# Latent-token MLPs by one level of Strassen's scheme, the context MLP apart

## The chip, the cores and the metric

The kernel runs on one core of a Trainium2 chip. TensorE (PE) multiplies matrices into PSUM; VectorE (DVE), ScalarE (ACT) and GpSimd (POOL) work on tiles of 128 partitions in SBUF and PSUM; SyncE (SP) issues the DMAs between DRAM and SBUF. The metric is the device time of one execution in microseconds, less being better.

## The reference

Two layers of attention and MLP over 1024 latent tokens and 256 context tokens, with a width of 1024 and a hidden width of 4096, all in fp32. What the change concerns is the MLP of each layer (layer 0 also updates the context, layer 1 does not):

```python
def _mlp(h, w1, w2):
    a = jax.nn.relu(h @ w1)
    return (a * a) @ w2

# in reference(), per layer i, after the attention part
hx = hx + gx1 * yx
hx = hx + gx2 * _mlp(_modulate(hx, norm2_g[i], sx2, cx2), mlp_w1[i], mlp_w2[i])
if with_ctx:                      # layer 0 only
    hc = hc + gc1 * yc
    hc = hc + gc2 * _mlp(_modulate(hc, norm2_g[i], sc2, cc2), mlp_w1[i], mlp_w2[i])
```

`_modulate` is an RMS norm with a scale and a shift per channel.

## The kernel before

Activations are kept transposed, channels on partitions. The tokens are three tiles: latents 0 to 511 (tile 0), latents 512 to 1023 (tile 1) and the context (tile 2, 256 columns). Every fp32 matrix product is made of three matmuls on fp32r parts: each operand x is split into xh (a cast) and xl = x − xh, and `mm3` (L223 to 226) adds wh·xh, wh·xl and wl·xh. `wload` (L210 to 221) loads 512 KB of weights (tile wst), casts them on ScalarE (L219, wh) and subtracts on VectorE (L220, wl).

The MLP (`mlp`) takes the 32 hidden blocks of 128 in groups of two. For each tile of tokens, the first matrix is 24 matmuls per hidden block into a PSUM bank (pj); ScalarE applies ReLU (L323), VectorE squares (L325), ScalarE casts (L328, ah), VectorE subtracts (L329, al). The second matrix is, for each of the 8 output blocks, 6 matmuls (2 hidden blocks × 3) into a bank m, which VectorE scales by the gate and adds into h, held in SBUF (L349). `mlp_phase` orders the groups: in layer 0 the first four groups run tiles 0 and 2 while tile 1 is normed, in layer 1 tile 0 alone; the context goes along with the latents in layer 0 and uses the same loaded weights. The last two groups finish tile 0 ahead of the rest, so that its next norm (layer 0, `after0`) or its output (layer 1, `final`) overlaps with the others; layer 1's last group is cut into two column halves.

Ahead of each MLP, the out-projection of tile 1 (`out_proj0`, `out_proj_blk`) takes each block of h from DRAM (hc), adds and writes it back (hD), and `load_h` loads h again, 2 MB per tile (L790). After layer 0's MLP come the value projections of layer 1 (`v_part`), interleaved with the norms of tiles 1 and 2. During layer 0's MLP eight pieces of the next layer's conditioning (`ada_piece`) are computed.

A scheduler fixes each engine's order of instructions when the program is built, from the order in the code, priorities and a simulated time; pools of tiles with a fixed number of buffers set how far an engine may run ahead. All loads and stores are issued from SP's one queue, in its order.

## Time and profile before

| | us |
|---|---|
| median of 3 runs | 3144.76 (3142.53 to 3146.78) |
| span of the profiled execution | 3138.9 |
| PE busy | 3059.8 (97%) |
| VectorE busy | 1888.8 (60%) |
| ScalarE busy | 1263.7 (40%) |
| GpSimd busy | 266.3 (8%) |

The span runs from the first to the last instruction of one profiled execution. A timed run is 5.9 us longer in the median, for what lies around the span. The mean rate of the transfers is 115 GB/s. A share of busy time is a mean over stages: the views used below are the windows (busy time of each engine in a stretch), the groups by line, the chain of waits followed back from the last instruction, the timeline, and the list of DMA issues.

### The profile page before, as it was taken

The numbers are of one execution on the slowest core, as the hardware profiler recorded it, in microseconds if no ns is written. First come the engines' busy times: TensorE is split into PE (matmuls) and PEld (weight loads), VectorE is DVE, ScalarE is ACT, GpSimd is POOL, SyncE is SP. The second block draws the span as 40 slices with busy tenths as digits, with TensorE's granted clock in tenths as the row PEclk, the third lists the DMA queues.
The fourth block names the chain that finished last, engine by engine and source line by source line (L and its number), as shares of the span: only waits on it lengthen the run. The fifth ranks groups of instructions, "written<-read, shape, count | busy, mean of one in ns | idle before, by whom it ended". The sixth has DMA issues, their size and how long they took to land.

```text
span 3138.9 us, 45259 instructions
## 1 busy us (share of the span) xinstructions
PE 3059.8 (97%) x17346; PEld 2540.1 (81%) x17346; DVE 1888.8 (60%) x4317; ACT 1263.7 (40%) x2430; POOL 266.3 (8%) x262
## 2 busy tenths in 40 slices
PE   8999999999999999999999999999999999999998
PEld 5876767668888888888899888888887788888887
DVE  4456775766754445445671568997785755455455
ACT  5345664643321121121352236897784322211122
POOL 0100120300000000000000222322120000000000
PEclk9999999999999999999999999999999999999999
DMA  8478674441221111210334357655534231111122
GB/s 309 146 225 247 188 202 141 146 166 56 77 85 54 55 54 54 67 54 27 108 124 130 130 164 213 145 127 136 154 86 155 89 98 49 47 48 50 45 69 86
DMA packets 139768, 361.57 MB, mean 115 GB/s; under 512 B 16288, under 2 KB 41504, under 8 KB 138400
## 3 DMA queue, kind: packets, MB, share of 16 engines
q1 hardware_dynamic: 139552, 358.69, 37.2%
q8 instruction: 136, 2.23, 0.3%
q14 instruction: 80, 0.66, 0.1%
HBM read 297.81 MB, written 58.20 MB: 113 GB/s over the span
## 4 chain that ended last, share of the span: by engine, by line
PE 88%; DMA 5%; DVE 4%; ACT 1%; issue 1%; SPq 0%; POOL 0%; DVEq 0%; POOLq 0%; ACTq 0%
PE pj L224 12%; PE pj L226 12%; PE pj L225 12%; PE m L225 8%; PE m L224 8%; PE m L226 8%; PE s L938 4%; PE pv L979 4%; PE pvp L613 2%; PE pt L609 2%; PE pt L974 2%; PE op L224 2%; PE op L225 2%; PE op L226 2%; PE pv L309 2%; PE pv L310 2%
## 5 line engine op out<-in xcount | busy, mean ns | idle before, releaser
L224 PE MATMUL pj<-yh,wh 128*128 128x512 f32 (+1 forms) x1840 | 684.8, 373 | 14.1 <-DVE hc L657 4.4
L226 PE MATMUL pj<-yh,wl 128*128 128x512 f32 (+1 forms) x1840 | 684.1, 372 | 0.7 <-DVE wl L220 0.7
L225 PE MATMUL pj<-yl,wh 128*128 128x512 f32 (+1 forms) x1840 | 681.8, 371 | 0.5 <-DVE yl L254 0.5
L219 ACT CAST wh<-wst 128x1024 fp32r<-128x1024 f32 x274 | 285.3, 1049 | 930.3 <-PE m L225 536.7
L220 DVE TENSOR_TENSOR wl<-wst,wh 128x1024 fp32r<-128x1024 f32 x274 | 334.8, 1229 | 422.8 <-ACT wh L219 421.5
L349 DVE SCALAR_TENSOR_TENSOR h<-m,ada,h 128x512 f32<-128x512 f32 (+1 forms) x648 | 432.9, 689 | 185.7 <-PE m L226 182.0
L225 PE MATMUL m<-al,wh 128*128 128x512 f32 (+1 forms) x1296 | 474.6, 367 | 0.2 <-DVE al L329 0.2
L226 PE MATMUL m<-ah,wl 128*128 128x512 f32 (+1 forms) x1296 | 473.8, 366 | 0.0
L224 PE MATMUL m<-ah,wh 128*128 128x512 f32 (+1 forms) x1296 | 437.0, 368 | 5.2 <-ACT ah L328 5.2
L224 PEld LDWEIGHTS pj<-yh,wh 128*128 128x128 f32 x1840 | 349.7, 190 | 81.3 <-issue 6.9
L226 PEld LDWEIGHTS pj<-yh,wl 128*128 128x128 f32 x1840 | 349.6, 190 | 63.7 <-DVE wl L220 1.5
L225 PEld LDWEIGHTS pj<-yl,wh 128*128 128x128 f32 x1840 | 349.5, 190 | 62.1 <-DVE yl L254 0.8
L224 PEld LDWEIGHTS m<-ah,wh 128*128 128x128 f32 x1296 | 243.3, 189 | 46.7 <-ACT ah L328 6.5
L225 PEld LDWEIGHTS m<-al,wh 128*128 128x128 f32 x1296 | 245.5, 189 | 40.5 <-DVE al L329 0.4
L226 PEld LDWEIGHTS m<-ah,wl 128*128 128x128 f32 x1296 | 245.3, 189 | 40.0
L945 DVE CUSTOM_DVE_ANT_0 p<-s,zero 128x512 f32<-128x512 f32 (+1 forms) x384 | 213.4, 596 | 34.1 <-POOL p L967 19.0
L938 PE MATMUL s<-kt,qt 128*128 128x512 f32 (+1 forms) x768 | 196.3, 376 | 6.1 <-DVE m L945 4.7
L325 DVE TENSOR_TENSOR s<-r 128x512 f32<-128x512 f32 (+1 forms) x160 | 101.3, 634 | 153.5 <-ACT r L323 153.4
L957 ACT ACTIVATE p<-p,nm 128x1280 f32<-128x1280 f32 x128 | 175.2, 1369 | 33.8 <-DVE nm L956 33.4
L979 PEld LDWEIGHTS pv<-v,pT 128*128 128x128 f32 x1280 | 161.5, 191 | 18.0 <-ACT pT L976 12.7
L979 PE MATMUL pv<-v,pT 128*128 128x128 f32 x1280 | 172.7, 275 | 2.4 <-ACT pT L976 2.4
L323 ACT ACTIVATE r<-pj 128x512 f32<-128x512 f32 (+1 forms) x160 | 88.1, 551 | 194.8 <-PE pj L226 193.1
(152 smaller groups left out, 4322.9 us busy)
## 6 DMA issues: line engine op xcount, KB each, us to landing
wst<-in_mlp_w_dram SPq DMA_DIRECT2D x176, 512.0 KB, 3.5
adaw<-in_ada_w_dram SPq DMA_DIRECT2D x96, 512.0 KB, 5.6
kt<-kD SPq DMA_DIRECT2D x32, 640.0 KB, 9.9
q<-qD SPq DMA_DIRECT2D x64, 256.0 KB, 6.2
qt<-rD SPq DMA_DIRECT2D x64, 256.0 KB, 7.2
wst<-in_even_w_out_dram SPq DMA_DIRECT2D x24, 512.0 KB, 4.6
wst<-in_odd_qk_dram SPq DMA_DIRECT2D x24, 512.0 KB, 4.4
v<-vD SPq DMA_DIRECT2D x16, 640.0 KB, 4.0
```

The lines of the kernel that those rows point to most:

```text
L219: act.copy(wh, st)
L220: dve.tensor_tensor(wl, st, f32(wh), op=OP.subtract)
L224: pe.matmul(out, lhsT=wh, rhs=xh, start=first, stop=False)
L225: pe.matmul(out, lhsT=wh, rhs=xl, start=False, stop=False)
L226: pe.matmul(out, lhsT=wl, rhs=xh, start=False, stop=last)
L323: act.activation(r[:, :w], ps[:, :w], AF.Relu)
L325: dve.tensor_tensor(s[:, :w], r[:, :w], r[:, :w], op=OP.mult)
L349: dve.scalar_tensor_tensor(h[t][:, blk, c0:c1], ps[:, : c1 - c0], ada[layer][:, 40 + blk, c : c + 1], h[t][:, blk, c0:c1], op0=OP.mult, op ...
L938: pe.matmul(S[:, :cw], lhsT=q[n][:, m, sl], rhs=kt[:, m, c0 : c0 + cw], start=(n == 0), stop=(n == 1),)
L945: dve.tensor_tensor_reduce(p[:, c0 : c0 + cw], S[:, :cw], zero.to_broadcast([P, cw]), 1.0, 3e38, OP.add, OP.min, accum_out=m3[:, ci : ci + 1],
L957: act.activation(p, p, AF.Exp, bias=nm, scale=-1.0, accum_out=s2[:, m : m + 1])
L979: pe.matmul(pv, lhsT=pT[:, j * P : j * P + P], rhs=v[:, c, :], start=(c == 0), stop=(c == 9))
```

## The change

The latents' MLPs are written as one level of the Strassen-Winograd scheme, over a 2 × 2 split: the tokens by tile (0, 1), the inner dimension in halves, the hidden blocks in pairs. Seven block products take the place of eight; their operands are sums and differences of blocks (S1 to S4 of activations, T1 to T4 of weights), and the results are put together from the products in X, Y, Z.

First matrix: for each pair of hidden blocks seven products of 12 matmuls. The combinations of activations are made once per layer (`comb_split`); those of the weights per pair on GpSimd (L448 to 451, L456), and each combination is split by ScalarE (L433) and VectorE (L434, tile wp). For the first 8 pairs of a layer two products that need tile 0 alone run early (`early1`), while tile 1 is normed, and their results go through DRAM. After ReLU and square, GpSimd makes S1 to S4 (L545 to 549) and all seven operands of the pair are stored to DRAM, 256 KB each (aD, L553).

Second matrix (`mlp2`): in groups of four pairs, seven operands per pair are loaded again (sa, L570) and split; each product is 4 blocks × 12 matmuls. VectorE (L590) and ScalarE (L594, L595) evict them, and GpSimd adds the shared parts into h (L596, L600, L603). h is loaded at the joint between the matrices (L708). The first group's weight sums run on VectorE. Layer 1's last pair stays a plain second matrix, cut as before.

The context's MLP in layer 0 runs after the latents', with its own loads of all weights; its 8 output blocks stay in four PSUM banks until the end. The norms of tiles 0 and 1 for layer 1 run beside it, and the value stage is reordered. The out-projection of tile 1 adds into tiles of SBUF that the norm then reads. A weight buffer more (st 4 for 3), and a scratch size for dynamic DMA of 2048.

The diff, cut to its core:

```diff
+EARLY = 8
+GROUPS = ((0, 1, 2, 3), (4, 5, 6, 7), (8, 9, 10, 11), (12, 13, 14, 15))
+GROUPS_LAST = ((0, 1, 2, 3), (4, 5, 6, 7), (8, 9, 10, 11), (12, 13, 14))
...
-    def mlp_phase(layer, xs, first, rest, h, y, after, cuts=None):
...
+    ORDER = (
+        ("A11", "B11", "X", True),
+        ("S2", "T2", "Y", True),
+        ("A12", "B21", "X", False),
+        ("S1", "T1", "Z", True),
+        ("S3", "T3", "Y", False),
+        ("S4", "B22", "Z", False),
+        ("A22", "T4", "Y", False),
+    )
+    wturn, turn2 = [0], [1]
...
+    def split_pair(src, tag):
+        w = M.tile([P, 2, 512], F32R, name="wp", tag=tag)
+        act.copy(w[:, 0, :], src)
+        dve.tensor_tensor(w[:, 1, :], src, f32(w[:, 0, :]), op=OP.subtract)
+        return w
...
+    def wsums(B11, B12, B21, B22, eng=pool):
+        T3 = M.tile([P, 512], F32, name="tw")
+        eng.tensor_tensor(T3, B22, B12, op=OP.subtract)
+        T2 = M.tile([P, 512], F32, name="tw")
+        eng.tensor_tensor(T2, T3, B11, op=OP.add)
+        eng.tensor_tensor(B12, B12, B11, op=OP.subtract)
+        return {"B11": B11, "B21": B21, "B22": B22, "T1": B12, "T2": T2, "T3": T3}
+
+    def woperand(W, n):
+        if n == "T4":
+            pool.tensor_tensor(W["T2"], W["B21"], W["T2"], op=OP.subtract)
+            return wsplit(W["T2"])
+        return wsplit(W[n])
...
+    def product1(ps, w, comb, first):
+        hi, lo = comb
+        for k in range(4):
+            sl = slice(k * P, k * P + P)
+            wh, wl = w[:, 0, sl], w[:, 1, sl]
+            acc = dict(skip_group_check=True)
+            pe.matmul(ps, lhsT=wh, rhs=hi[:, k, :], start=first and k == 0, stop=False, **acc)
+            pe.matmul(ps, lhsT=wh, rhs=lo[:, k, :], start=False, stop=False, **acc)
+            pe.matmul(ps, lhsT=wl, rhs=hi[:, k, :], start=False, stop=k == 3, **acc)
...
+    def early1(layer, p, comb):
+        st = wraw(ap["mlp_w1"][layer, 2 * p], "st")
+        ps = PS.tile([P, 512], F32, name="X", tag=mmt())
+        product1(ps, wsplit(st[:, :512]), comb["A11"], True)
+        r = tmp("R", "er")
+        act.copy(r, ps)
+        sp.dma_start(rD1[p], r)
+        product1(ps, wsplit(st[:, 512:]), comb["A12"], False)
+        a = tmp("a11", "er")
+        act.activation(a, ps, AF.Relu)
+        act.activation(a, a, AF.Square)
+        sp.dma_start(aD[p, "A11"], a)
...
+    def prep1(layer, p):
+        st = [wraw(ap["mlp_w1"][layer, 2 * p + i], "st") for i in range(2)]
+        W = wsums(st[0][:, :512], st[1][:, :512], st[0][:, 512:], st[1][:, 512:])
+        if p < EARLY:
+            W["R"], W["A11"] = tmp("R", "ta"), tmp("a11", "ta")
+            sp.dma_start(W["R"], rD1[p])
+            sp.dma_start(W["A11"], aD[p, "A11"])
...
+    def mlp1(layer, p, comb, plain, W):
...
+        for an, bn, bank, first in ORDER:
+            if done and bank == "X":
+                continue
+            if first:
+                ps[bank] = PS.tile([P, 512], F32, name=bank, tag=mmt())
+            x = ps[bank]
+            product1(x, woperand(W, bn), comb[an], first)
+            if bn == "B11":
+                R = tmp("R", "ta")
+                act.copy(R, x)
+            elif bn == "T2":
+                U = tmp("U", "ta")
+                dve.tensor_tensor(U, x, R, op=OP.add)
+            elif bn == "B21":
+                a["A11"] = tmp("a11", "ta")
+                act.activation(a["A11"], x, AF.Relu)
+                act.activation(a["A11"], a["A11"], AF.Square)
+            elif bn == "T1":
+                V = tmp("V", "ta")
+                dve.tensor_tensor(V, x, R, op=OP.add)
+            elif bn == "T3":
+                dve.tensor_tensor(V, x, V, op=OP.add)
+                square_relu(V)
+                a["A22"] = V
+            elif bn == "T4":
+                dve.tensor_tensor(R, x, R, op=OP.add)
+                square_relu(R)
+                a["A21"] = R
+            else:
+                dve.tensor_tensor(U, x, U, op=OP.add)
+                square_relu(U)
+                a["A12"] = U
+        if plain:
+            names = {"A11": a["A11"], "A12": a["A12"], "A22": a["A22"], "S1": a["A21"]}
+        else:
+            S1, S2 = tmp("S1", "ta"), tmp("S2", "ta")
+            pool.tensor_tensor(S1, a["A21"], a["A22"], op=OP.add)
+            pool.tensor_tensor(S2, S1, a["A11"], op=OP.subtract)
+            pool.tensor_tensor(a["A21"], a["A11"], a["A21"], op=OP.subtract)
+            S4 = tmp("S4", "ta")
+            pool.tensor_tensor(S4, a["A12"], S2, op=OP.subtract)
+            names = {"A11": a["A11"], "A12": a["A12"], "A22": a["A22"], "S1": S1, "S2": S2, "S3": a["A21"], "S4": S4}
+        for n, x in names.items():
+            if not (done and n == "A11"):
+                sp.dma_start(aD[p, n], x)
+
+    def mlp2(layer, group, h, load=None):
+        W = {}
+        for p in group:
...
+            W[p] = wsums(
+                st[0][:, :512], st[0][:, 512:], st[1][:, :512], st[1][:, 512:], dve if load else pool
+            )
+        ps, R, U, V = {}, {}, {}, {}
+        for an, bn, bank, first in ORDER:
+            ops = []
+            turn2[0] += 1
+            for p in group:
+                x = M.tile([P, 512], F32, name="sa")
+                sp.dma_start(x, aD[p, an])
+                ops.append((woperand(W[p], bn), split_pair(x, f"as{turn2[0] % 2}")))
+            if load and first:
+                load()
+                load = None
+            for blk in range(4):
+                if first:
+                    ps[bank, blk] = PS.tile([P, 512], F32, name=bank, tag=mmt())
+                x = ps[bank, blk]
+                sl = slice(blk * P, blk * P + P)
+                for i, (w, a) in enumerate(ops):
+                    acc = dict(skip_group_check=True)
+                    last = i == len(ops) - 1
+                    pe.matmul(x, lhsT=w[:, 0, sl], rhs=a[:, 0, :], start=first and i == 0, stop=False, **acc)
+                    pe.matmul(x, lhsT=w[:, 0, sl], rhs=a[:, 1, :], start=False, stop=False, **acc)
+                    pe.matmul(x, lhsT=w[:, 1, sl], rhs=a[:, 0, :], start=False, stop=last, **acc)
...
+                def add(out, g, other):
+                    dve.scalar_tensor_tensor(out, x, g, other, op0=OP.mult, op1=OP.add)
+
+                if bn == "B11":
+                    Ra, R[blk] = tmp("Ra", "ru"), tmp("R", "ru")
+                    act.activation(Ra, x, AF.Copy, scale=g0)
+                    act.activation(R[blk], x, AF.Copy, scale=g1)
+                    pool.tensor_tensor(h[1][:, blk, :], h[1][:, blk, :], Ra, op=OP.add)
+                elif bn == "T2":
+                    U = tmp("U", "ru")
+                    add(U, g1, R[blk])
+                    pool.tensor_tensor(h[0][:, blk + 4, :], h[0][:, blk + 4, :], U, op=OP.add)
+                elif bn == "T3":
+                    add(R[blk], g1, R[blk])
+                    pool.tensor_tensor(h[1][:, blk + 4, :], h[1][:, blk + 4, :], R[blk], op=OP.add)
+                else:
+                    t, b, g = {
+                        "B21": (0, blk, g0),
+                        "T1": (1, blk + 4, g1),
+                        "T4": (1, blk, g0),
+                        "B22": (0, blk + 4, g1),
+                    }[bn]
+                    add(h[t][:, b, :], g, h[t][:, b, :])
+
...
+    def mlp_x(layer, work, tags, left):
...
+        def first():
+            yield from raw_norm(layer, 0, y0, "pt")
+            for n, k0 in (("A11", 0), ("A12", 4)):
+                for k in range(4):
+                    comb_split(comb, n, k, y0[k0 + k])
...
+        for p in range(EARLY):
+            early1(layer, p, comb)
+            next(steps, None)
...
+        for k in range(4):
+            S1, S2 = tmp("S1", "tmp"), tmp("S2", "tmp")
+            dve.tensor_tensor(S1, y1[k], y1[k + 4], op=OP.add)
+            dve.tensor_tensor(S2, S1, y0[k], op=OP.subtract)
+            comb_split(comb, "S2", k, S2)
+            pool.tensor_tensor(y0[k], y0[k], y1[k], op=OP.subtract)
+            pool.tensor_tensor(y0[k + 4], y0[k + 4], S2, op=OP.subtract)
+            comb_split(comb, "S1", k, S1)
+        for k in range(4):
+            comb_split(comb, "S3", k, y0[k])
+        for k in range(4):
+            comb_split(comb, "A22", k, y1[k + 4])
...
+        groups = GROUPS if layer == 0 else GROUPS_LAST
+        W = prep1(layer, 0)
+        for p in range(16):
+            now, W = W, prep1(layer, p + 1) if p < 15 else None
+            mlp1(layer, p, comb, layer == 1 and p == 15, now)
...
+        h = {t: M.tile([P, KC, 512], F32, name=f"h{t}") for t in range(2)}
+
+        def load():
+            for t in (1, 0):
+                sp.dma_start(h[t], hD[t])
+
+        for g in groups:
+            mlp2(layer, g, h, load if g is groups[0] else None)
+        return h
...
-    def out_proj0(t, blk, tag="mx"):
+    def out_proj0(t, blk, tag="mx", hc=None):
...
+    h = mlp_x(
+        0,
+        [lambda hc, op=op, tag=tag: out_proj0(*op, tag, hc) for op, tag in zip(ops, OPT0)],
...
+    def ctx_mlp(after):
+
+        out = [PS.tile([P, 512], F32, name=f"o{i}", tag="mm") for i in range(4)]
...
+        a = hidden(0)
+        for f in range(NFF):
+            a, (ah, al) = hidden(f + 1) if f < NFF - 1 else None, a
+            wh, wl = wload(ap["mlp_w2"][0, f * P : f * P + P, :], P)
+            for blk in range(KC):
+                ps = out[blk // 2][:, blk % 2 * 256 : blk % 2 * 256 + 256]
+                for w, x in ((wh, ah), (wh, al), (wl, ah)):
...
+            after(f)
...
+    def between(f):
+        if f in (0, 12):
+            between.steps = norm1(f // 12)
+            save(f // 12)
+        next(between.steps, None)
+
+    ctx_mlp(between)
...
+    h = mlp_x(
+        1,
+        [lambda hc, blk=blk, tag=tag: out_proj_blk(1, blk, tag, hc) for blk, tag in enumerate(OPT1)],
...
-    mlp_phase(1, XS1, [0], [1], h, y, lambda: final(0, range(4)), cuts)
...
+        for n in (("A11", "A12"), ("S1", "A22"))[t]:
+            x = M.tile([P, 512], F32, name="fo")
+            sp.dma_start(x, aD[15, n])
+            a[t].append(split_pair(x, "ap"))
+    mlp2_plain(1, 15, h, 0, a[0], W, [(0, 512, lambda: final(0, range(4)))])
+    mlp2_plain(1, 15, h, 1, a[1], W, cuts)
```

VectorE, in layer 0's second matrix. Before, the end of one group's evictions of tile 0 or 1 and the splits of the next group's weights and activations (wl of weights, s and al of activations):

```order
L349 SCALAR_TENSOR_TENSOR h_8223<-m_9728,ada_142,h_8223 128x512
L349 SCALAR_TENSOR_TENSOR h_8223<-m_9736,ada_142,h_8223 128x512
L220 TENSOR_TENSOR wl<-wst,wh 128x1024 x2
L325 TENSOR_TENSOR s<-r 128x512
L329 TENSOR_TENSOR al<-s,ah 128x512
L220 TENSOR_TENSOR wl<-wst,wh 128x1024
L325 TENSOR_TENSOR s<-r 128x512
L329 TENSOR_TENSOR al<-s,ah 128x512
L220 TENSOR_TENSOR wl<-wst,wh 128x1024
L349 SCALAR_TENSOR_TENSOR h_8223<-m_9834,ada_142,h_8223 128x512
L349 SCALAR_TENSOR_TENSOR h_8223<-m_9842,ada_142,h_8223 128x512
```

VectorE, in layer 0's second matrix after the change, where splits of weights (from wst) and of reloaded activations (from sa) go to tiles wp, and evictions of bank Y into U:

```order
L434 TENSOR_TENSOR wp<-wst,wp 128x512
L434 TENSOR_TENSOR wp<-sa,wp 128x512
L590 SCALAR_TENSOR_TENSOR U<-Y,ada_262,R 128x512
L434 TENSOR_TENSOR wp<-wst,wp 128x512
L434 TENSOR_TENSOR wp<-sa,wp 128x512
L590 SCALAR_TENSOR_TENSOR U<-Y,ada_262,R 128x512 x2
L434 TENSOR_TENSOR wp<-wst,wp 128x512
L434 TENSOR_TENSOR wp<-sa,wp 128x512
L434 TENSOR_TENSOR wp<-wst,wp 128x512
L590 SCALAR_TENSOR_TENSOR U<-Y,ada_262,R 128x512
L434 TENSOR_TENSOR wp<-sa,wp 128x512
```

One eviction now stands between two to four splits of half the width, and the operands of the product that follows are split while the present one is evicted.

GpSimd, in layer 0's MLP before: between the sums of masks of the attention (L751) and the rotary sums of layer 1 (L283) only the small steps of the norms stand.

```order
L751 TENSOR_TENSOR bm<-nmask,bt 128x384 x64
L232 TENSOR_TENSOR rs<-ms,mhalf 128x4
L232 TENSOR_TENSOR rs<-ms,mhalf 128x2
L232 TENSOR_TENSOR rs<-ms,mhalf 128x4 x2
L232 TENSOR_TENSOR rs<-ms,mhalf 128x2
L232 TENSOR_TENSOR rs<-ms,mhalf 128x4
L283 TENSOR_TENSOR s<-s,sinT 128x512 x26
```

GpSimd, in layer 0's second matrix after the change: additions into h (h_11112 is tile 1, h_11111 tile 0), and between them the weight sums T3, T2 and T1 of the next group.

```order
L596 TENSOR_TENSOR h_11112<-h_11112,Ra 128x512 x4
L600 TENSOR_TENSOR h_11111<-h_11111,U 128x512 x4
L448 TENSOR_TENSOR tw<-wst 128x512
L450 TENSOR_TENSOR tw<-tw,wst 128x512
L451 TENSOR_TENSOR wst<-wst 128x512
L448 TENSOR_TENSOR tw<-wst 128x512
L450 TENSOR_TENSOR tw<-tw,wst 128x512
L451 TENSOR_TENSOR wst<-wst 128x512
L603 TENSOR_TENSOR h_11112<-h_11112,R 128x512 x3
```

28 such sums stand in each group of four pairs, where there was nothing.

SP's queue, layer 0, before: h of tile 1 ahead of the weights, then weights with nothing but the conditioning's weights between them.

```order
L216 DMA wst<-in_mlp_w_dram 128x1024
L790 DMA h_8223<-hD_73 128x4096
L216 DMA wst<-in_mlp_w_dram 128x1024 x29
L166 DMA adaw<-in_ada_w_dram 128x1024 x2
L216 DMA wst<-in_mlp_w_dram 128x1024 x4
L166 DMA adaw<-in_ada_w_dram 128x1024 x2
```

SP's queue, layer 0 after the change, at the joint between the two matrices (aD14 and aD15 are the last pairs' operands on their way to DRAM, sa the first group's on their way back):

```order
L553 DMA aD14S_219<-R 128x512
L553 DMA aD14S_220<-S_10917 128x512
L708 DMA h_11112<-hD_73 128x4096
L553 DMA aD15A_221<-a_10977 128x512
L553 DMA aD15A_223<-V 128x512
L570 DMA sa<-aD0A_116 128x512
L553 DMA aD15A_222<-U 128x512
L570 DMA sa<-aD1A_123 128x512
L570 DMA sa<-aD2A_130 128x512
```

The load of h for tile 1 now stands ahead of the first four loads of activations, and two of the last pair's stores between them.

## Rows read from the trace of the kernel before

**Rows 1.** The page: totals of the engines; shares of the chain of waits.
```profile
PE 3059.8 (97%) x17346; PEld 2540.1 (81%) x17346; DVE 1888.8 (60%) x4317; ACT 1263.7 (40%) x2430; POOL 266.3 (8%) x262
...
PE 88%; DMA 5%; DVE 4%; ACT 1%; issue 1%; SPq 0%; POOL 0%; DVEq 0%; POOLq 0%; ACTq 0%
```

**Rows 2.** Windows: PE, weight loads, VectorE, ScalarE, GpSimd (instructions), clock, DMA share, GB/s.
```profile
0.00:78.00 78.00, 63.67 (x411) 46.28 (x412) 34.33 (x68) 41.98 (x77) 6.00 (x13) 0.91 0.83 311
...
392.00:470.00 78.00, 71.63 (x531) 47.05 (x523) 60.58 (x219) 52.00 (x124) 20.27 (x20) 0.96 0.72 205
...
706.00:1600.00 894.00, 890.47 (x4721) 757.72 (x4722) 491.73 (x744) 218.69 (x336) 2.63 (x3) 1.00 0.19 63
...
2412.00:3139.00 727.00, 710.79 (x3166) 585.01 (x3164) 395.75 (x533) 180.24 (x261) 5.76 (x9) 0.99 0.21 69
...
2420.00:2430.00 10.00, 7.94 (x29) 6.04 (x28) 5.82 (x9) 5.74 (x10) 0.00 (x0) 0.83 0.33 129
...
2600.00:2700.00 100.00, 100.00 (x438) 81.93 (x437) 47.55 (x61) 20.93 (x29) 0.00 (x0) 1.00 0.15 48
```

**Rows 3.** Chain (start us, us, what): two successive groups, layer 1's MLP.
```profile
2513.13 1.62 PE m L224 x7
...
2535.26 1.62 PE m L224 x7
```

**Rows 4.** Timeline of PE, matmuls on 256 columns: start us, us.
```profile
1608.66 0.28 PE L309 MATMUL pv<-wl,yh 128*128 128x256 f32 x1
1608.78 0.28 PE L310 MATMUL pv<-wh,yl 128*128 128x256 f32 x1
```

**Rows 5.** Groups by line and form: busy us, mean ns; idle before, releaser.
```profile
L349 DVE SCALAR_TENSOR_TENSOR h<-m,ada,h 128x512 f32<-128x512 f32 x504 | 365.9, 748 | 159.4 <-PE m L226 155.9
...
L220 DVE TENSOR_TENSOR wl<-wst,wh 128x1024 fp32r<-128x1024 f32 x274 | 334.8, 1229 | 422.8 <-ACT wh L219 421.5 <-DMA vD<-vev 0.9
...
L329 DVE TENSOR_TENSOR al<-s,ah 128x512 fp32r<-128x512 f32 x128 | 88.3, 690 | 68.3 <-ACT ah L328 68.0
...
L328 ACT CAST ah<-s 128x512 fp32r<-128x512 f32 x128 | 79.4, 621 | 153.9 <-DVE s L325 153.9
...
L323 ACT ACTIVATE r<-pj 128x512 f32<-128x512 f32 x128 | 75.9, 593 | 165.5 <-PE pj L226 164.7 <-DVE al L329 0.6
```

**Rows 6.** Line 283 on GpSimd: ns least, median, most; first and last start us.
```profile
L283 POOL TENSOR_TENSOR s<-s,sinT x38: 1280/1736/2094, 48.4 to 1958.0; 128x512 f32<-128x512 f32 x38
```

**Rows 7.** Timeline of GpSimd and VectorE at three places of layer 1.
```profile
1798.42 0.69 DVE L284 TENSOR_TENSOR q<-q,cosT 128x512 f32<-128x512 f32 x1
...
1798.46 1.80 POOL L283 TENSOR_TENSOR s<-s,sinT 128x512 f32<-128x512 f32 x1 [6.54 <-DVE s L282]
...
1898.31 1.29 POOL L283 TENSOR_TENSOR s<-s,sinT 128x512 f32<-128x512 f32 x1 [9.76 <-DVE s L282]
...
1907.63 1.16 POOL L967 TENSOR_TENSOR p<-p 128x448 f32<-128x448 f32 x1 [8.03 <-ACT p L966]
1907.66 0.68 DVE L945 CUSTOM_DVE_ANT_0 p<-s,zero 128x512 f32<-128x512 f32 x1
...
1908.74 2.09 POOL L283 TENSOR_TENSOR s<-s,sinT 128x512 f32<-128x512 f32 x1
...
1909.78 1.60 DVE L284 TENSOR_TENSOR q<-q,cosT 128x512 f32<-128x512 f32 x1
```

**Rows 8.** DMA issues: count, KB each, median us from issue to landing.
```profile
hc<-hD SPq DMA_DIRECT2D x32, 256.0 KB, 3.5
hD<-hc SPq DMA_DIRECT2D x32, 256.0 KB, 3.0
h<-hD SPq DMA_DIRECT2D x4, 2048.0 KB, 9.2
```

**Rows 9.** Chain of waits from the out-projection into layer 1's MLP.
```profile
2412.96 9.64 DMA h<-hD
...
2424.40 2.74 PE m L224 x8
2427.14 0.43 PE m L225
2427.56 0.43 PE m L226
```


## The prediction before the run

> **What bounds the kernel now.** First the totals of the page: PE is busy for 97% of a span of 3138.9 us, VectorE for 60% of it, GpSimd for 8%, and the chain of waits followed back from the end is 88% PE and 5% DMA [rows 1]. So time is won where matmuls go, provided nothing else comes late. Then the windows by stage: the latent MLP of layer 1 lies in 2412 to 3139 with PE busy 710.8 of 727 us, layer 0's MLP in 706 to 1600 with 890.5 of 894; in a quiet stretch of it PE has all 100 us at full clock, VectorE 47.6, GpSimd nothing, and the transfers need 48 GB/s [rows 2]. Then the chain inside that stretch, for the price of one matmul: from one start of a group's second-matrix matmuls to the next are 22.13 us [rows 3], and one group of two hidden blocks on one tile of 512 tokens issues 2 × 8 × 3 matmuls of the first matrix and 8 × 2 × 3 of the second, 96, so 0.2305 us each. On 256 columns they start 0.12 us apart [rows 4].
>
> **What goes.** Matmuls on latent tiles in both MLPs: before 2 layers × 2 tiles × 32 blocks × 48 = 6144, of which the end of layer 1 cuts 48 into 96 of half the columns: 6096 of 512 columns and 96 halves. After: first matrix 16 pairs × 7 products × 12 = 1344 per layer; second matrix 1344 in layer 0 and 1260 in layer 1, whose last pair stays plain with 48 and 96 halves. That is 5340, or 756 fewer. 756 × 0.2305 = 174.3 us of PE. The context's 1536 matmuls of 256 columns are as many as before, and cost the same if their operands come in time.
>
> **What comes, by stage.** Durations of 128x512 pieces: a split's subtraction 0.69 us on VectorE, an eviction that multiplies and adds 0.75, a cast on ScalarE 0.62, an eviction there 0.59 [rows 5]; a sum of two SBUF tiles on GpSimd 1.28 at its shortest [rows 6].
>
> *First matrix.* A full pair is 84 matmuls, 19.4 us; VectorE has 7 splits and 5 evictions, 4.8 + 3.8 = 8.6 us; GpSimd 4 sums of weights and 4 of activations, 8 × 1.28 = 10.2. A half pair (the first 8 of a layer, whose first two products ran early) has 60 matmuls, 13.8 us, against VectorE's 5 splits and 5 evictions, 7.2, and GpSimd's same 10.2. ScalarE with 5 to 7 casts and 6 or so passes stays near 8 us.
>
> *Second matrix.* A group of 4 pairs is 7 products × 4 blocks × 12 = 336 matmuls, 77.4 us. VectorE: 28 weight splits and 28 of reloaded activations, 56 × 0.69 = 38.6, and 24 evictions × 0.75 = 18.0: 56.6 us. GpSimd: 12 sums, 4 for T4, 12 additions into h: 28 × 1.28 = 35.8. ScalarE: 56 × 0.62 + 8 × 0.59 = 39.4. Each alone fits.
>
> *The two together.* VectorE and GpSimd hinder each other: where they overlap, GpSimd's sum takes 1.80 and 2.09 us against 1.29 alone, and VectorE's multiplication 1.60 against 0.69; a VectorE pass that reads PSUM went through in 0.68 beside a GpSimd instruction [rows 7]. The price of a GpSimd sum to VectorE has never been seen back to back. It lies between 0 (it falls into VectorE's waits or beside an eviction) and 1.28 (VectorE stands for all of it). The nearest row is the 1.60: 0.91 lost. I take 0.85, a little less since 24 of the 80 VectorE instructions of a group are evictions. A group then has 56.6 + 28 × 0.85 = 80.4 us on VectorE against 77.4 on PE, 3.0 late, × 7.75 groups = 23 us; a half pair 7.2 + 6.8 = 14.0 against 13.8, 0.2 × 16 = 3; a full pair 15.4 against 19.4, nothing. In general, with x us per sum, the loss is 7.75 × (28x − 20.8) + 16 × (8x − 6.6) = 345x − 267, as long as the brackets are positive.
>
> The Trainium skill ("SBUF — State Buffer", section "SBUF: two separate sides") says that the port pair which VectorE and GpSimd share is an exclusive lock: a VectorE instruction with two SBUF inputs and a GpSimd instruction that reads SBUF wait for each other for the whole instruction. By that rule the sums and the splits of a group would stand one behind the other, an estimate of 38.6 + 35.8 = 74.4 of 77.4 us, with the evictions of PSUM beside them: it would just fit, and the term of 23 us would be near 0. The trace agrees as far as [rows 7] go: 1.80 against 1.29, and 0.68 unhindered.
>
> *Set-up of the combinations*, once per layer: about 55 VectorE instructions (38 to 40 us, and the sums on GpSimd beside them) against 8 × 24 early matmuls × 0.2305 = 44 us. It nearly hides; I charge 4 us per layer (0 to 15).
>
> *Joint from first to second matrix.* All transfers pass SP's one queue in order. What is queued ahead of the second matrix's first activations is h of one tile (2 MB) and the last pair's stores; PE has only the last pair's 36 to 48 matmuls, 8 to 11 us, for that. A 2 MB load needs 9.2 us from issue, 9.64 in the chain; a 256 KB load 3.5, a store 3.0 [rows 8, 9]. Four activation loads and their splits follow, some 3.5 + 2 × 0.69 until the first is ready. Nothing of this wait is in the trace of before. Bounds 0 (issued early enough) to 15 (9.6 + 3.5 + 1.4). I take 8 per layer, 16. After a wait of this kind the granted clock fell: a mean of 0.83 in the ten microseconds around the joint in layer 1 [rows 2], with matmuls 0.43 us apart for a while, as at the lower of the two levels [rows 9]; that is in the 8.
>
> *Other joints.* Out-projection to early products: before it costs a few microseconds (h is loaded for 9.64 us ahead of the first MLP matmul [rows 9]); the operands now need one split more, 3 per layer, 6 in all (−4 to 15). Start of the context MLP: norm, new operands and first weights with no latent work left to cover, 8 us, and 4 within it. Inside, a block is 48 × 0.12 = 5.8 us of PE against 2 × 1.23 for two weight splits [rows 5], at most 2 × 0.69 for the half-size activation and some 0.7 for the norms run beside it, 4.5 us of VectorE, and 2 × 512 KB of weights, 182 GB/s; 205 was sustained in a stretch of layer 0 [rows 2]. So the context's own 64 weight loads, which it shared with the latents before, are hidden; without that cover they would be 64 × 1.23 = 79 us. End of layer 1: the plain pair 15 reloads and splits its activations behind the last group, 6. Sum 16 + 6 + 12 + 6 = 40 (0 to 75). Tile 1's out-projection result stays in SBUF and needs no reload; PE had no idle time behind those reloads, so I give it nothing. The value stage is only reordered: the same matmuls, nothing.
>
> *Transfers.* A half pair loads 1 MB of weights and 2 × 256 KB and stores 6 × 256 KB: 3.15 MB in 13.8 us, 228 GB/s. That is above the 205 of the stretch just named and below the 311 of the start [rows 2]. I charge nothing; at 205 it is 15.4 us, 1.6 × 16 = 25.
>
> **Sum.** 3138.9 − 174.3 + 23 + 3 + 8 + 40 = 3038.6 for the span. The median of the three runs, 3144.76, stands 5.9 above the span of the profiled one; with that 3044.5.
>
> **Rivals.**
> 1. *All hidden.* The sums fall into VectorE's waits, x near 0, and the joints cost half: 3138.9 − 174.3 + 4 + 20 + 5.9 = 2994. For it: VectorE's 57 of 77 us and queues that run one product ahead. Against it: two engines with 56.6 and 35.8 us in 77.4 that can't both read, and evictions that wait for PE's last matmul. Chance 0.11.
> 2. *VectorE becomes the bound.* x of 1.05 to 1.28. The durations counted back to back are some 0.08 too long, 80 × 0.08 = 6.4 us per group, so with x = 1.28 a group has 86 us, 8.6 × 7.75 = 67, a half pair 16.6, 2.8 × 16 = 45: 3138.9 − 174.3 + 67 + 45 + 48 + 5.9 = 3130. For it: the 0.91 of the one clean pair, and GpSimd at 2.09. Chance 0.15 for 3090 to 3138.
> 3. *Slower than before*: the same price at its full length with no part beside evictions, in the second matrix and the half pairs. It decides where 345x − 267 + 48 passes 174.3, at x = 1.14; at 1.28 it gives 3138.9 − 174.3 + 175 + 48 + 5.9 = 3193. For it: GpSimd's longest sums of 2.09 show that it gives way as well, so that VectorE may wait for a lengthened sum. Against it: a third of VectorE's work reads PSUM. Chance 0.12, of which 0.02 lies within the bound of no change.
> 4. *Transfers bound the half pairs*: 25 us more, 3070, with a store waiting at the head of SP's queue ahead of the next weights. It lies in the forecast's own range, 0.05 of its chance.
>
> **How the numbers follow.** Forecast with rival 4: 0.62, own range 2995 to 3090. Rival 1 0.11, rival 2 0.15, rival 3 0.12. About 0.2% (6 us) is what a measurement of this kernel can tell from none. Faster 0.62 + 0.11 + 0.14 = 0.87, same 0.02, slower 0.11. The range from 2990 to 3130 leaves out most of rival 3 and half of rival 1.
>
> **What would show it.** PE's 512-column matmuls down by 756 and its busy time by about 174 us. In a group of the second matrix PE near 77 us, the windows there with VectorE above 70 of 77 and PE waiting on splits (operands "wp") rather than on transfers; GpSimd's sums between 1.3 and 2.1 us, VectorE's splits at a mean of 0.8 to 1.3. At each layer's joint one wait of 5 to 10 us on activations behind h. The context MLP near 190 us, with PE above 90%. The forecast is wrong if PE is above 97% in the second matrix (rival 1), if splits wait for GpSimd on the chain of waits for over 10 us a group (rivals 2 and 3), or if the half pairs stand on weight loads at some 200 GB/s (rival 4).

## The result: 0.9% faster, a quarter of what was forecast

| | median of 4 runs, us | ratio to before, 95% interval |
|---|---|---|
| before | 3143.65 (3137.88 to 3146.78) | |
| after | 3115.97 (3110.99 to 3124.14) | 0.9911 (0.9885 to 0.9937) |

That is 28 us where the forecast had 100. The profiled execution of the changed kernel is the longest of the four, 3124.14 us, its span 3122.4. First the totals and the chain of its page, which answer to [rows 1]:

```profile
PE 2943.0 (94%) x16590; PEld 2416.6 (77%) x16590; DVE 2086.6 (67%) x4413; ACT 1601.8 (51%) x3134; POOL 964.0 (31%) x726
...
PE 77%; DVE 7%; DMA 6%; POOL 3%; issue 3%; ACT 2%; SPq 1%; DVEq 0%; POOLq 0%; ACTq 0%
```

PE has 756 matmuls fewer, as counted, but its busy time fell by 117 us and not by 174, and its idle time rose from 79 to 179 us. So 57 us more went into the matmuls that are left and 100 into waits: −174 + 57 + 100 = −17, the difference of the two spans. Most of the 57 is the clock. Its mean fell from 0.990 to 0.974: it was granted at the lower of its two levels, half, for 163 us in place of 65, and PE was busy for 129 and 54 us of these, so about 38 us more are lost at half speed. The other 19 are not told apart. The chain of waits gave PE 88% before and gives it 77% now, with VectorE, GpSimd and DMA in the gap. Where that is, the windows tell (columns as in [rows 2]):

```profile
740.00:758.00 18.00, 7.41 (x23) 5.27 (x21) 16.18 (x13) 10.23 (x19) 17.92 (x11) 0.72 0.21 64
...
800.00:890.00 90.00, 85.50 (x413) 64.89 (x412) 48.19 (x65) 39.15 (x65) 56.18 (x40) 0.97 0.63 218
...
1088.00:1106.00 18.00, 15.23 (x51) 11.60 (x52) 13.88 (x14) 6.26 (x12) 10.45 (x7) 0.78 0.54 177
1106.00:1400.00 294.00, 293.12 (x1294) 242.40 (x1293) 267.52 (x313) 135.32 (x251) 148.51 (x96) 1.00 0.49 152
1400.00:1420.00 20.00, 11.13 (x60) 9.87 (x59) 13.36 (x26) 9.48 (x19) 0.71 (x1) 0.74 0.48 177
1420.00:1608.00 188.00, 186.08 (x1537) 185.55 (x1536) 127.39 (x176) 100.69 (x155) 2.02 (x2) 0.99 0.55 175
...
2457.00:2480.00 23.00, 13.12 (x47) 9.67 (x46) 21.03 (x17) 14.35 (x27) 21.60 (x13) 0.85 0.28 102
...
2811.00:3075.00 264.00, 264.00 (x1166) 218.48 (x1165) 242.16 (x280) 114.38 (x210) 129.93 (x86) 1.00 0.42 131
```

The second matrix (1106 to 1400, 2811 to 3075), where the forecast saw the danger, runs at PE's speed: 264.00 of 264 us, a matmul every 0.2264 us, though VectorE is busy for 91% of it. The time is lost ahead of it, in the first matrix: at its start (740 to 758, 2457 to 2480) GpSimd is busy for 17.9 of 18 and 21.6 of 23 us, VectorE nearly as long, and PE for half. The same from the waits of PE, the largest of the whole span (total, times, longest):

```profile
PE X L471 <- ACT R L487: 18.4, 5, 7.8
PE Y L471 <- DVE U L521: 15.3, 7, 3.2
PE Z L471 <- ACT wp L433: 11.3, 16, 0.7
PE X L583 <- ACT wp L433: 9.9, 2, 5.2
```

The first three are of the first matrix (L471), the fourth is the joint, once per layer, 5 us each. The chain through layer 1's start shows who holds the first (start us, us, what):

```profile
2452.83 7.51 POOL y0a L673
2460.36 0.63 ACT s3h L462
2461.01 1.09 DVE s3l L463
2462.10 1.68 DVE s2l L463
2463.78 1.68 DVE s1l L463
2465.46 0.61 ACT s2h L462
2466.07 0.50 ACT a L491
2466.57 0.48 ACT R L487
...
2470.53 1.72 POOL y0b L674
2472.25 1.69 POOL tw L448
2474.01 1.62 POOL tw L450
2475.63 1.68 POOL wst L451
2477.31 1.71 POOL tw L448
...
2479.66 1.68 POOL tw L456
```

In ScalarE's order the copy R, for which X of the early products waits, stands behind the cast of S3 (s3h), and that cast waits for GpSimd's first sum, y0a (timeline of ScalarE and PE):

```profile
2460.36 0.62 ACT L462 CAST s3h<-y0a 128x512 fp32r<-128x512 f32 x1 [4.72 <-POOL y0a L673]
...
2467.10 0.79 PE L471 MATMUL X<-a12h,wp 128*128 128x512 f32 x1 [7.55 <-ACT R L487]
```

The combinations (L673, L674) and the first pairs' weight sums (L448 to L456) stand in one line on GpSimd, 30 us almost without a pause from 2452.8 on. Most take 1.6 to 1.7 us, where [rows 6] had 1.28 at best, and splits of 0.69 [rows 5] take 1.68 beside them. But the first of them took 7.5 us, in both layers. The timeline of the two engines shows what ran beside it (start us, us):

```profile
2452.80 7.53 POOL L673 TENSOR_TENSOR y0a<-y0a,y1a 128x512 f32<-128x512 f32 x1 [18.41 <-DVE S L671]
2460.29 1.27 POOL L674 TENSOR_TENSOR y0b<-y0b,S 128x512 f32<-128x512 f32 x1
```

```profile
2453.10 0.68 DVE L463 TENSOR_TENSOR a22l<-y1b,a22h 128x512 fp32r<-128x512 f32 x1
2453.70 0.68 DVE L434 TENSOR_TENSOR wp<-wst,wp 128x512 fp32r<-128x512 f32 x1
...
2458.52 0.68 DVE L670 TENSOR_TENSOR S<-y1a,y1b 128x512 f32<-128x512 f32 x1
2461.01 1.09 DVE L463 TENSOR_TENSOR s3l<-y0a,s3h 128x512 fp32r<-128x512 f32 x1 [1.81 <-ACT s3h L462]
```

VectorE went through ten instructions without a pause, 0.60 us apart from 2453.10 to 2458.52, each with two SBUF inputs and each at its full speed of 0.68. GpSimd's sum ended 1.1 us after the last of them, when VectorE had stopped for lack of input; S3's cast and split then need that sum. In the 17 us that follow VectorE doesn't pause either, yet there the two engines take turns, some 1.7 us for each instruction. Why this sum waited out ten and the later ones one each, the trace doesn't show.

Measured on PE's matmuls in each trace, by stage (floor: the matmuls at 0.2305 us in the first matrix, 0.2264 in the second, and some 10 us of conditioning in layer 0's first):

| us | floor | after | e1 | e2 | e3 | e11 |
|---|---|---|---|---|---|---|
| first matrix with early part, layer 0 | 320 | 378 | 365 | 358 | 342 | 355 |
| the same, layer 1 | 310 | 368 | 357 | 356 | 339 | 355 |
| joints, both | 0 | 10 | 10 | 7 | 22 | 6 |
| second matrix, layer 0 | 304 | 312 | 312 | 309 | 307 | 306 |
| second matrix, layer 1 | 285 | 289 | 287 | 290 | 287 | 290 |

The first matrix is 116 us above its floor, the second some 11. Where the 116 lie shows when the first matrix's matmuls are counted off in order, 192 of the early part, 480 of the half pairs, 672 of the full ones in each layer (a few change places at the borders):

| above the floor, both layers, us | after | e1 | e2 | e3 | e11 |
|---|---|---|---|---|---|
| early part and set-up | 47 | 26 | 25 | 38 | 24 |
| half pairs | 32 | 30 | 20 | 10 | 18 |
| full pairs | 37 | 37 | 38 | 3 | 38 |

e1 to e11 are the experiments.

### The profile page after: what moved, and what is told of

Same layout as the page of the kernel before. It is cut to its first block, busy times and chain, and to the rows that moved or that the text cites. A ratio compares the mean times of both kernels' runs of the same rounds, so it can differ in the third digit from the quotient of the medians.

```text
span 3122.4 us, 46912 instructions
## 1 busy us (share of the span) xinstructions
PE 2943.0 (94%) x16590; PEld 2416.6 (77%) x16590; DVE 2086.6 (67%) x4413; ACT 1601.8 (51%) x3134; POOL 964.0 (31%) x726
## 4 chain that ended last, share of the span: by engine, by line
PE 77%; DVE 7%; DMA 6%; POOL 3%; issue 3%; ACT 2%; SPq 1%; DVEq 0%; POOLq 0%; ACTq 0%
PE pv L1311 4%; PE s L1270 4%; PE pj L230 4%; PE pj L232 4%; PE pj L231 4%; PE o L1156 3%; PE Y L583 3%; PE Y L584 3%; PE Y L585 3%; PE pvp L916 2%; PE Y L471 2%; PE Y L473 2%; PE Y L472 2%; PE pt L912 2%; PE op L230 2%
## 5 line engine op out<-in xcount | busy, mean ns | idle before, releaser
L434 DVE TENSOR_TENSOR wp<-wst,wp 128x512 fp32r<-128x512 f32 x252 | 220.7, 879 | 139.4 <-ACT wp L433 139.4
L433 ACT CAST wp<-wst 128x512 fp32r<-128x512 f32 x252 | 155.0, 620 | 269.0 <-PE Z L585 86.1
L230 PE MATMUL pj<-yh,wh 128*128 128x512 f32 (+1 forms) x816 | 281.2, 346 | 10.8 <-ACT wh L225 6.4
L231 PE MATMUL pj<-yl,wh 128*128 128x512 f32 (+1 forms) x816 | 280.3, 344 | 1.1 <-DVE yl L260 1.1
L232 PE MATMUL pj<-yh,wl 128*128 128x512 f32 (+1 forms) x816 | 280.2, 344 | 0.6 <-DVE wl L226 0.6
L433 ACT CAST wp<-tw 128x512 fp32r<-128x512 f32 x189 | 115.5, 619 | 270.1 <-PE Y L473 116.2
L434 DVE TENSOR_TENSOR wp<-tw,wp 128x512 fp32r<-128x512 f32 x189 | 208.5, 1111 | 32.2 <-ACT wp L433 31.8
L434 DVE TENSOR_TENSOR wp<-sa,wp 128x512 fp32r<-128x512 f32 x217 | 211.1, 977 | 5.3 <-ACT wp L433 5.3
L230 PEld LDWEIGHTS pj<-yh,wh 128*128 128x128 f32 x816 | 157.4, 193 | 32.3 <-ACT wh L225 7.7
L1311 PEld LDWEIGHTS pv<-v,pT 128*128 128x128 f32 x1280 | 161.3, 191 | 19.4 <-ACT pT L1308 14.3
L231 PEld LDWEIGHTS pj<-yl,wh 128*128 128x128 f32 x816 | 157.6, 193 | 19.2 <-DVE yl L260 1.6
L232 PEld LDWEIGHTS pj<-yh,wl 128*128 128x128 f32 x816 | 157.2, 193 | 19.1 <-DVE wl L226 1.0
L433 ACT CAST wp<-sa 128x512 fp32r<-128x512 f32 x217 | 133.6, 619 | 37.7 <-PE Y L585 12.9
```

The costliest lines, as they stand in the source:

```text
L230: pe.matmul(out, lhsT=wh, rhs=xh, start=first, stop=False)
L231: pe.matmul(out, lhsT=wh, rhs=xl, start=False, stop=False)
L232: pe.matmul(out, lhsT=wl, rhs=xh, start=False, stop=last)
L433: act.copy(w[:, 0, :], src)
L434: dve.tensor_tensor(w[:, 1, :], src, f32(w[:, 0, :]), op=OP.subtract)
L1311: pe.matmul(pv, lhsT=pT[:, j * P : j * P + P], rhs=v[:, c, :], start=(c == 0), stop=(c == 9))
```

## Experiments

Theory A: the first matrix stands on GpSimd's sums, at its start and in the half pairs. Theory B, the forecast's: VectorE is held up by GpSimd in the second matrix. Theory C: weights and stores come late through SP's queue. All ratios are to the kernel before, run beside them (its medians were 3147.6 to 3148.2).

**e1, the combinations' sums on VectorE.**

```diff
-            pool.tensor_tensor(y0[k], y0[k], y1[k], op=OP.subtract)
-            pool.tensor_tensor(y0[k + 4], y0[k + 4], S2, op=OP.subtract)
+            dve.tensor_tensor(y0[k], y0[k], y1[k], op=OP.subtract)
+            dve.tensor_tensor(y0[k + 4], y0[k + 4], S2, op=OP.subtract)
```

> The 8 sums per layer that make the combinations S3 and S4 of the activations (lines 673 and 674) run on VectorE instead of GpSimd; all else is as in the changed kernel, 3116 us. Theory A (the first matrix starts late because its operands stand in one chain on GpSimd, 8 sums for the combinations and then the first pairs' weight sums, some 1.7 us each): the wait between the early products and the first pair shrinks in both layers, 3090 to 3106 us. Theory B (the forecast's: the time is lost to VectorE being held up by GpSimd in the second matrix): within 6 us of 3116. Theory C (weights and stores late in SP's queue): within 8 us of 3116, the waits being filled by transfers.

3094.64 us, ratio 0.9832 (0.9817 to 0.9847). Moving 16 instructions of 464 brings 0.8%, as A said; the first matrix is 23 us shorter over both layers, 22 of them in the early part and set-up, and PE's waits of X on the copy R (L487) go from 7.8 us in layer 0 and 10.6 in layer 1 to 4.7 and 3.5. B and C don't have it.

**e2, all sums of the first matrix on VectorE.**

```diff
-        W = wsums(st[0][:, :512], st[1][:, :512], st[0][:, 512:], st[1][:, 512:])
+        W = wsums(st[0][:, :512], st[1][:, :512], st[0][:, 512:], st[1][:, 512:], dve)
...
-            pool.tensor_tensor(S1, a["A21"], a["A22"], op=OP.add)
+            dve.tensor_tensor(S1, a["A21"], a["A22"], op=OP.add)
```

(and so T4 and S2 to S4, with e1.)

> All sums of the first matrix, those of the combinations, of the weights (T1 to T4) and of the activations (S1 to S4), run on VectorE; GpSimd works in the second matrix alone. VectorE has then some 0.6 us more per sum, about 12 us in a half pair of 14. Theory A: 3070 to 3095 us, the half pairs at 14 us each without waits. Theory B: within 8 us of 3116. Theory C: the waits of the half pairs stay, 3095 to 3112 us.

3084.43 us, 0.9801 (0.9784 to 0.9817): in A's range, but only 0.3% beyond e1. These 10 us are of the half pairs, which still stand 20 above their floor; the full pairs gain nothing. The waits on U (L522 there) went from 9.8 us in the changed kernel to 6.4 in layer 0 and from 5.5 to 9.0 in layer 1. So moving the sums to VectorE takes a part of the wait away, and a part stays.

**e3, those sums left out** (T1 to T4 and S1 to S4; the combinations stay on GpSimd).

```diff
+        W["T2"], W["T3"], W["T4"], W["raw"] = W["B11"], W["B22"], W["B21"], True
...
+            S1, S2, S4 = a["A21"], a["A11"], a["A12"]
```

> Leaves out the sums of weights and of activations in the first matrix (T1 to T4 and S1 to S4 are taken as plain blocks, so the results differ from the reference); the combinations at the start stay on GpSimd. Loads, stores, splits and matmuls are as many as before. It bounds what these sums cost, on whatever engine: theory A 3070 to 3095 us; theory C 3100 to 3112 us, since loads and stores stay; theory B within 6 us of 3116.

3059.05 us, 0.972 (0.9701 to 0.9739), more than any theory said. Its windows in half and full pairs:

```profile
800.00:870.00 70.00, 70.00 (x350) 53.80 (x349) 31.30 (x56) 34.07 (x57) 0.00 (x0) 1.00 0.75 262
...
900.00:1020.00 120.00, 120.00 (x517) 96.79 (x516) 49.71 (x74) 58.23 (x99) 0.00 (x0) 1.00 0.44 147
```

PE has no wait while the transfers run at 262 GB/s, more than the 218 of the changed kernel's half pairs. So as a matter of rate C falls for the pairs: loads and stores would be in time. Of the first matrix's 116 us, the sums with all that waits for them are 65 (746 − 681), 34 of them in the full pairs, where moving the sums gained nothing. Their buffers and their places in the engines' orders go with them, which e3 doesn't tell apart.

What e3 doesn't clear either is the order of SP's queue. In the changed kernel's half pairs of layer 0 (770 to 910 us) SP stands on sums and activations that its next store (L553) or the next weight buffer (L443) needs, and the loads behind wait with it (SP's waits: total, times, longest):

```profile
SPq L443 <- POOL tw L456: 19.9, 7, 6.6
SPq L553 <- POOL S L545: 19.4, 5, 9.8
SPq L553 <- ACT V L477: 15.0, 4, 7.8
```

Loads of weights are 9.5% of the chain of waits there (772 to 910 us), and 12.7% in e2 (750 to 881). How much of the half pairs' loss comes through such late loads no run shows.

**e6, Strassen's scheme in layer 1 alone** (layer 0 and the value stage as before, with four load buffers).

```diff
+    mlp_phase(0, XS0, [0, 2], [1], h, y, after0)
...
     h = mlp_x(
         1,
```

> Strassen's scheme in layer 1 alone; layer 0 with the context in its MLP as in the kernel before (four load buffers as after the change). From the two traces the MLP of layer 1 gained 24 us and lost up to 8 ahead of it: 3119 to 3130 us if the two layers add up, and layer 0's share of the gain (latents and context together) is then 0 to 15 us. If the layers were to hinder each other, it would be outside that.

3125.63 us, 0.9931 (0.9916 to 0.9946). Layer 1 alone gives 22 us of the 28; layer 0 with both parts of the change about 6.

**e12, the context's MLP apart, alone** (all else as before the change).

```diff
-    mlp_phase(0, XS0, [0, 2], [1], h, y, after0)
+    mlp_phase(0, XS0, [0], [1], h, y, after0)
...
+    ctx_mlp(lambda f: None)
```

> The kernel before (ratio 1) with the second part of the change alone: the latents' MLP of layer 0 plain as before, the context's MLP behind it with its own 64 weight loads and its output in four PSUM banks; the norms of the context and of tile 0 stay where they were. Theory: within the stage VectorE, ScalarE and the transfers keep up (in the changed kernel's trace the inner part runs at 186 of 188 us), so the part costs only its start, 0 to 12 us, ratio 1.000 to 1.004. Rival (the context in the latents' groups filled PE's waits there and shared weights): 15 to 40 us, ratio 1.005 to 1.013.

3164.88 us, 1.0057 (1.0036 to 1.0078): 17 us slower, at the lower end of what the rival said. It has neither the norms beside the context nor the reordered value stage. If the parts add, Strassen's scheme brings 28 − 22 + 17 = 23 us in layer 0, about what it brings in layer 1, and this part takes all but 6 of them back; each of the three numbers has an interval of 5 to 8 us to either side.

**e7, a fifth buffer for the split weights**, against the third wait above.

```diff
-    M.open("right", st=4, wh=4, wl=4)
+    M.open("right", st=4, wh=5, wl=5)
```

> Five buffers in place of four for each of the two tags of split weights; else the changed kernel (ratio to the kernel before 0.9911). In its full pairs PE waits 0.7 us in each for the cast of T1, and that cast starts when a product just before has ended. If the cast waits for a buffer of the split weights, the wait goes: 16 x 1.1 us (with the gaps behind it), ratio about 0.986. If it waits for its place in ScalarE's order or for something else, the ratio stays at 0.989 to 0.993.

0.9898 (0.988 to 0.9917): nothing to be told from the change itself. The wait of Z on the cast is nearly gone from its trace (1.4 us in 2 waits, where it was 11.3 in 16), and another stands in its place, in layer 0 and again in layer 1:

```profile
PE X L471 <- ACT R L518: 10.0, 6, 2.7
```

PE waits for a copy instead, 20.0 us over both layers where it was 5.2; that the order fixed at build time changes with the buffers is the likely reason, not a shown one. What makes the cast late in the changed kernel isn't settled.

**e9, the context's first norm steps ahead of the last group.**

```diff
+            if ahead and g is groups[-1]:
+                ahead(h)
             mlp2(layer, g, h, load if g is groups[0] else None)
```

> The load of the context's h and the first two steps of its norm (squares, sum, transposes, reciprocal root) are put ahead of the last group of the second matrix in layer 0; else the changed kernel. Theory: at the start of the context MLP PE has nothing else to do while the norm runs (9 us idle and about 5 more at the lower clock, from 1400 to 1420 us in its trace); with the steps moved 5 to 9 us go, ratio 0.9885 to 0.9895. Rival (the first weights and the operands' splits come last anyway): within 0.1% of 0.9911.

0.9889 (0.9872 to 0.9906). It points the way the theory said, but the intervals overlap.

**e11, all sums of both matrices on VectorE.**

```diff
-                    pool.tensor_tensor(h[1][:, blk, :], h[1][:, blk, :], Ra, op=OP.add)
+                    dve.tensor_tensor(h[1][:, blk, :], h[1][:, blk, :], Ra, op=OP.add)
```

(and so the other additions into h and the second matrix's weight sums, with e2.)

> All sums of both matrices on VectorE, GpSimd free of them: 56.6 us of VectorE in a group of the second matrix become 56.6 + 28 x 0.6 = 73 by pitch against 76 of PE. If a GpSimd sum costs VectorE about as much as the sum itself would (the two exclude each other), the time is that of e2 within 0.3%, ratio 0.977 to 0.983. If GpSimd's sums ran for free beside VectorE, this takes VectorE to its limit and loses 5 to 25 us against e2, ratio 0.982 to 0.988. Rival, the forecast's price of 0.85 us on VectorE per GpSimd sum: faster than e2 by 10 us or more, below 0.977.

3080.18 us, 0.9792 (0.9776 to 0.9808), within 0.1% of e2: neither the loss of sums that ran for free nor the gain that the forecast's 0.85 us would give. The splits by form (busy, mean ns), in the changed kernel:

```profile
L434 DVE TENSOR_TENSOR wp<-wst,wp 128x512 fp32r<-128x512 f32 x252 | 220.7, 879 | 139.4 <-ACT wp L433 139.4
...
L434 DVE TENSOR_TENSOR wp<-sa,wp 128x512 fp32r<-128x512 f32 x217 | 211.1, 977 | 5.3 <-ACT wp L433 5.3
...
L434 DVE TENSOR_TENSOR wp<-tw,wp 128x512 fp32r<-128x512 f32 x189 | 208.5, 1111 | 32.2 <-ACT wp L433 31.8
```

and in e11:

```profile
L434 DVE TENSOR_TENSOR wp<-wst,wp 128x512 fp32r<-128x512 f32 x252 | 172.4, 688 | 64.5 <-ACT wp L433 64.5
...
L434 DVE TENSOR_TENSOR wp<-sa,wp 128x512 fp32r<-128x512 f32 x217 | 148.4, 687 | 2.6 <-ACT wp L433 2.5
...
L434 DVE TENSOR_TENSOR wp<-tw,wp 128x512 fp32r<-128x512 f32 x189 | 128.6, 687 | 11.1 <-ACT wp L433 11.1
```

Beside GpSimd the 658 splits take 640.3 us, alone 449.4: 191 us for 464 sums, 0.41 us of VectorE per GpSimd sum. With the other VectorE instructions that both kernels have it is 215 us, 0.46. The page of e11 has VectorE's busy time at

```profile
PE 2915.4 (95%) x16590; PEld 2398.3 (78%) x16590; DVE 2146.1 (70%) x4877; ACT 1601.6 (52%) x3134; POOL 267.1 (9%) x262
```

where it was 2086.6 us: 464 sums more cost it 60 us, 0.13 each. In e11's second matrix VectorE does every sum itself and is less busy than in the changed kernel, where GpSimd did them:

```profile
1070.00:1361.00 291.00, 291.00 (x1285) 240.98 (x1284) 253.91 (x405) 131.68 (x245) 0.00 (x0) 1.00 0.48 152
```

That is 87% against 91% (267.52 of 294), with 405 instructions against 313.

**e10, e13: put together.** e10 is e2 with e7 and e9; e13 is e11 with e9.

> The first matrix's sums on VectorE (as in e2, ratio 0.9801), five buffers of split weights and the context's norm ahead of the last group, all together. If the three gains are of different waits they add: 0.9801 less 0.005 less 0.002, 0.973. If VectorE has become the bound of the first matrix, the buffers bring nothing there: 0.977 to 0.980.

> All sums on VectorE (as e11, ratio 0.9792) and the context's load and first norm steps ahead of the last group of layer 0's second matrix (as e9). If the two are independent: 0.977. If the last group has no room on VectorE for the norm's sums: 0.979 to 0.981.

e10: 3083.98 us, 0.9805 (0.9783 to 0.9827); the gains don't add, and its trace has a wait of 16.8 us on a cast at layer 0's joint, 3.6 in e2. e13: 3074.52 us, 0.9767 (0.9749 to 0.9786), the fastest of those that make every sum, faster than both kernels: 73 us under the one before. Against e11 it is 0.0025 less, as e9 was 0.0022 less than the change, neither clear by itself.

**e14, e15: 4 and 12 early pairs in place of 8**, on e11.

```diff
-EARLY = 8
+EARLY = 4
```

> All sums on VectorE (as e11) and 4 early pairs per layer in place of 8. Half pairs are now 4 and full ones 12. Theory D (half pairs cost about 2 us each beyond their matmuls, the norm of tile 1 and the set-up are covered by the early products): 4 x 12 x 2 matmuls or 22 us less cover per layer, of which the half pairs give back 8: ratio 0.983 to 0.988. Theory E (the early products bring nothing, since the set-up waits for VectorE and ScalarE which they load themselves): 0.974 to 0.980.

> All sums on VectorE (as e11) and 12 early pairs per layer: 22 us more cover per layer for the norm of tile 1 and the set-up, 4 more half pairs. In e11's trace some 10 us per layer of PE's waits and low clock lie in that stretch. Theory D: ratio 0.974 to 0.979. Theory E, or the extra trips through DRAM making the half pairs late: 0.980 to 0.985.

e14: 3109.92 us, 0.9879 (0.9853 to 0.9904), 0.9% slower than e11: the early products do cover the norm and the set-up, as D said. e15: 3090.72 us, 0.982 (0.9796 to 0.9843), slower too: the first matrix is 13 and 5 us longer in the two layers, so D's other half, that more cover helps, is wrong. Counted off as above, the start is no shorter (24 us above its floor in e15 as in e11), and PE's waits on U go from 15.6 us to 30.9: the loss lies in the pairs, as the second reason given for E has it. Whether the extra trips through DRAM make them late wasn't tried apart.

## Why the prediction was wrong

Right were the count and price of what goes (756 matmuls, and a pitch of 0.226 to 0.232 us), the sign, the size of the joint (5 us of wait in each layer, and a clock of 0.78 in the 18 us behind it in layer 0, where the forecast had 8), and that VectorE and GpSimd hinder each other.

**The step that failed** is the cost of the first matrix: 3 us for the half pairs, 8 for the set-up, 6 for the joint ahead of it and nothing for the full pairs, 17 in all. It measured 116 above its floor: 47 in the early part and set-up where the forecast had 14, 32 in the half pairs for 3, 37 in the full pairs for nothing. Two errors stand in it.

- The set-up was weighed as VectorE's work against the early matmuls (38 to 40 us against 44), with "the sums on GpSimd beside them". GpSimd was not given its own line: 8 combinations and the first pairs' weight sums, 30 us from 2452.8 on, which begin when tile 1 is normed, and behind which ScalarE's copies for the early products stand. e1 shows it: with 8 sums per layer on the other engine the 47 us become 26 and the whole time falls by 25.
- In the pairs each engine's work was summed and compared with PE's, and all but fitted (GpSimd 10.2 and VectorE 14.0 of 13.8 us in a half pair, 15.4 of 19.4 in a full one). But a pair is a chain: load, sum of T3, T2, T1, cast, split, product, eviction, two passes of ScalarE, sums of S, store. The sums stand on that chain on whichever engine they are: e2 moves them and gains 10 us more, e3 leaves them out and gains 35 beyond e1, with PE at 70.00 of 70 us in half pairs and 120.00 of 120 in full ones. Which link of the chain holds PE in the full pairs is open (see e7). What the sum of busy times can't show is the wait, and after each wait the clock: 0.72 in the 18 us at the start.

**Terms that were too large.** The second matrix was charged 23 us for 0.85 us of VectorE per GpSimd sum, taken from one pair of rows [rows 7]; 0.41 to 0.46 was measured and VectorE still fitted, so the term is near 0. It also counted 28 GpSimd sums in the first group of each layer, which has 16. By the exclusive lock that the Trainium skill states ("SBUF — State Buffer", section "SBUF: two separate sides") the prediction had an estimate of 74.4 of 77.4 us for that stage, so no loss; in the outcome the trace agrees, with PE busy for 264.00 of 264 us. Rivals 2 and 3 fall with this term. By its own sign, PE above 97%, rival 1 was right about the second matrix; its 2994 us are further off than the forecast, since it too gave the first matrix next to nothing. Of rival 4 the rate falls by e3; its store at the head of SP's queue isn't ruled out.

**Terms that were too small.** The context: 12 forecast, 17 in e12, and in the changed kernel's trace 208 us from 1400 to 1608 against 1536 × 0.12 = 184; most of it at the start, where PE has 11.1 of 20 us and a clock of 0.74. The inner part was forecast to need 182 GB/s and runs at 175 with PE at 99%.

The balance, from the profiled executions, where 3122.4 − 3038.6 = 84 us are missing (72 by the medians): the first matrix 117 − 17 = 100 more, with the conditioning at the 9 us that it took before; joints and second matrix 611 us, where the forecast had 2604 × 0.2305 + 23 + 16 = 639, so 29 less; the context 12 more; the last pair and the end 7 more; the stages outside the MLPs 14 more, most of it of this execution, the longest of four (in e11 the same stages are 2 us longer than before). Against these stand waits that the kernel before had in its own MLPs and that the sum left standing: 8 us over its matmuls in layer 0's MLP and 13 in layer 1's. 100 − 29 + 12 + 7 + 14 − 21 = 83.

What stays open: of the first matrix's 116 us, 51 are there without any sum of weights or activations (e3), 38 of them at each layer's early part and between it and the first pairs, where the norm of tile 1, the combinations and the first splits share VectorE and ScalarE. The combinations stay on GpSimd in e3; e1, which moves them, leaves 26 there. e14 and e15, made on e11, show that neither fewer nor more early pairs help. No run left out the sums and moved the combinations too.

## What to carry to other kernels

When work is moved to a second engine, follow one item through all engines in order of time, at the start of the stage above all, and give each engine its own line there; busy shares that fit say nothing on that. A scheme that saves matmuls pays in sums: here the first matrix's 252 sums of weights and activations took back some 60 us, a third of the 174 saved (e3), and where two engines hinder each other, the idle engine is no free place for them. Split a change into its parts before judging it: one part here cost 17 us that the other earned.

## What the runs showed of the hardware

A GpSimd sum of two 128x512 SBUF tiles took VectorE 0.41 us on the mean (e11 against the changed kernel), in splits that went from 0.688 to between 0.88 and 1.11 us, and was itself 1.32 to 1.61 us long, as the mean of each line but L673, in place of 1.28 at its shortest. Beside ten VectorE instructions without a pause one such sum took 7.5 us and didn't slow them, once in each layer; in the 17 us after it (layer 1) the two engines took turns, some 1.7 us for each instruction. Done by VectorE, a sum is some 0.6 us by pitch. So in this kernel a sum on GpSimd freed VectorE of 0.13 us (by its busy time) to 0.2 of these 0.6, and of nothing in the second matrix (91% busy with the sums on GpSimd, 87% without).
